# Native fp32 products with plain reads and strided writes, later feed-forward norm sums, and two attention products with other waits

## The chip, the core and the metric

The kernel runs on one core of one Trainium2 chip. The metric is device time in microseconds (us) of one execution. The core's engines are TensorE (PE, matmuls; PEld is its weight load), VectorE (DVE), ScalarE (ACT), GpSimd (POOL) and SyncE (SP, which issues the DMAs). SBUF is the on-chip memory that the engines read, PSUM the eight banks that PE writes.

## The reference

Two transformer-like blocks run one after the other on 256 positions of width 1024, all in fp32. Cut to what matters here:

```python
def hybrid_layer(x, ...):                       # first block
    proj = rms_norm(x, norm1_g) @ w_in
    ...                                         # three attentions, a short convolution, gates
    x = x + mixed @ w_out
    h = rms_norm(x, norm2_g)
    return x + jnp.square(jax.nn.relu(h @ w_up)) @ w_down

def second_block(x, mem, ...):
    z = _rmsnorm(h, norm_mix_g[l]) @ w_in[l]    # conv a and gate, q, k, v, index heads, two gates
    y_conv = _conformer_conv(c_a, c_g, ...) 
    y_attn = _dsa_attention(q, k, v, qi, ki, wi) @ w_attn_out[l]
    h = h + (g_conv * y_conv + g_attn * y_attn) @ w_mix_out[l]
    h = h + _cross_attention(_rmsnorm(h, norm_x_g[l]), _rmsnorm(mem, norm_mem_g[l]), ...)
    hf = _rmsnorm(h, norm_ffn_g[l]) @ w_ff1[l]
    h = h + jnp.square(jax.nn.relu(hf)) @ w_ff2[l]
    return _rmsnorm(h, norm_final_g)
```

The norm in front of each feed-forward half divides every position by the root of its mean square. The kernel multiplies by that factor after the two products, since ReLU and square let a positive factor through; so the factor is needed only when the second product is read out.

## The kernel before, in words

**Weights.** Nearly all weights come as units of 1 MB, 128 partitions by 2048 columns: four blocks of 128 rows of the product by 512 output features. `Stream` loads them through SP's queue in the order of use (line 108), three raw buffers `wr` deep. Each is then split in two: ACT rounds it to fp32r (`wh`, line 125) and DVE subtracts to get the rest (`wl`, line 126), in two halves per unit. Three split buffers exist, and when PE begins a unit the splits of the two units behind it have been asked for. A product of fp32 accuracy is then three fp32r matmuls (`mm3`, lines 261 to 263): high weights by high activations, high by low, low by high.

**Native units.** Four units (`NATIVE`, numbers 81, 85, 89 and 97 in the order) are not split: PE multiplies them in plain fp32 (line 290; line 343 for a token product), which the hardware runs as two matmul instructions per call. All four lie in the second block, where the long convolution loads ACT and DVE: unit 81 is the first half of the first 512 query features, 85 the same of the keys, 89 of the values (the token product), 97 of the second gate.

**Turned columns.** The matmuls of a feature product (`Feat`) read the 256 positions of an activation in the order 0, 128, 1, 129, ... (`turns`) and write PSUM columns one after the other. Whoever reads the PSUM tile out does it through `plain`, which undoes the order. A native unit is the first half of its product; the second half, split, adds onto the same PSUM tile in turned order.

**Order of the work.** PE's order is the order in which the program is written (`manual_schedule`). The other engines' queues are ordered by a planner, by priority and by its own estimate of times; what generators ask for has a priority 400 instructions ahead. Work beside the products is written as Python generators: `pump()` is called twice per unit, after half of it and at its end, and lets each generator run to its next `yield`. A unit is 48 matmuls of 256 columns, so a pump comes every 24 of them. What a generator asks PE for stands in PE's stream at the pump that runs it.

**Feed-forward sums.** `ffn_up` (both blocks) starts `norm_side`, then multiplies with the up weights: the first two groups of 512 features as a pair, the rest one after the other, two units each. `norm_side` asks for the squares and their folds (`sq_sum`, lines 409 to 419: two ACT instructions, four DVE ones) and, some pumps later, for the column sums on PE (`col_stats`, line 427), the scale and power on DVE and POOL, and in the first block, one pump on, for a broadcast by PE (line 457). In the second block `to_tokens` transposes `x` in four steps at the tenth to thirteenth pump, with an ACT copy each (line 1337). The tiles of 4 KB per partition (`H4`) share 24 slots.

**Attention products.** `heads_pv` (line 1010) multiplies transposed probabilities with values for two heads into a bank `po`, from which ACT (line 1015) and DVE (line 1016) make a high and a low half. In the second block's causal attention the loop over eight chunks runs one step per pump beside the gate products; scores (line 1069), transposes (line 1000) four steps later (`LAG2`), and the product with the values one step after those. Its output bank is the one bank of pool `pso`. In the cross attention four such products follow each other directly, in banks of `pss` (three banks) and `pso` by turns; right behind them comes the output projection, which reads `ch`, the halves that they leave. The pool `psm` has four banks, for the large products.

Of the kernel before, what the change touches and what calls it, by code (L numbers as in the profile page):

```python
# [9 lines left out]
F32 = mybir.dt.float32  # L10
# [6 lines left out]
T = 256  # L17
# [130 lines left out]
LAG2 = 4  # L148
# [10 lines left out]
def hybrid_conformer_kernel(ctx, tc, stop, dbg, xT, memT, wall, wtok, wkiwi, wcmp, par_d, cst_d, gfin_d, out):  # L159
    nc = tc.nc  # L160
    V, A, G, P = nc.vector, nc.scalar, nc.gpsimd, nc.tensor
# [4 lines left out]
    psm = ctx.enter_context(tc.tile_pool(name="psm", bufs=4, space=bass.MemoryType.PSUM))  # L166
    pss = ctx.enter_context(tc.tile_pool(name="pss", bufs=3, space=bass.MemoryType.PSUM))
    pso = ctx.enter_context(tc.tile_pool(name="pso", bufs=1, space=bass.MemoryType.PSUM))
# [21 lines left out]
    def PS(name="s"):  # L190
        return pss.tile([128, 512], F32, name=name, tag="s")
# [13 lines left out]
    def turns(ap):  # L205

        return ap.rearrange("p (s a) -> p a s", s=2)

    def plain(ps):

        return ps.rearrange("p n (a s) -> p n s a", s=2)
# [9 lines left out]
    def v3(ap):  # L221
        return ap.rearrange("p (s a) -> p s a", s=2)
# [42 lines left out]
    class Feat:  # L265
# [7 lines left out]
        def chunk(self, c):  # L273
            if self.ps is None:
                self.ps = [psm.tile([128, 2, T], F32, name="m", tag="m") for _ in range(2)]
            ps, act = self.ps, self.act
            wh, wl = W.next()
            wh = wh.rearrange("p (k o) -> p k o", k=4)
            if wl is not None:
                wl = wl.rearrange("p (k o) -> p k o", k=4)  # L280
            ks = self.kts[4 * c:4 * c + 4]
            end = c == self.nch - 1

            def one(kk, o):
                k = ks[kk]
                sl = slice(o * 128, o * 128 + 128)
                first = c == 0 and kk == 0 and o % 2 == 0
                last = end and kk == 3
                if wl is None:
                    P.matmul(out=ps[o // 2][:, o % 2].rearrange("p (a s) -> p a s", s=2), lhsT=wh[:, kk, sl], rhs=turns(act.raw(k)), start=first, stop=last, skip_group_check=True)  # L290
                else:
                    mm3(ps[o // 2][:, o % 2], wh[:, kk, sl], wl[:, kk, sl], act.hi(k), act.lo(k), first, last)

            if not end or self.kmajor:
                for kk in range(4):
                    for o in range(4):
                        one(kk, o)
                    if kk == 1:
                        pump()
                if end:  # L300
                    for b in range(2):
                        self.evac(plain(ps[b]), 2 * b, 2)
            else:
                for b in range(2):
                    for kk in range(4):
                        for o in (2 * b, 2 * b + 1):
                            one(kk, o)
                    self.evac(plain(ps[b]), 2 * b, 2)
                    if b == 0:
                        pump()  # L310
            pump()
# [92 lines left out]
    def sq_sum(src, name):  # L404

        sqs = []
        for hf in range(2):
            sq = H4(name="sq")
            A.activation(out=sq, in_=src[hf], func=AF.Square)
            sqs.append(sq)  # L410
        return fold(sqs)
# [62 lines left out]
    with tc.manual_schedule(engines=MANUAL):  # L474
# [399 lines left out]
        def ffn_up(act, src, tagr, bcast):  # L874
            res = {}

            def norm_side():
                for _ in range(5):
                    yield
                s = sq_sum(src, "s")  # L880
                yield
                yield
                ps = col_stats(s)
                r = rstd_col(ps, D, "r" + tagr)
                r2 = const.tile([128, 2], F32, name="rsq" + tagr)
                V.tensor_tensor(r2, r, r, op=ALU.mult)
                res["col"] = r2
                if not bcast:
                    return
                dg = col_diag(r2)  # L890
                yield
                ps = diag_bcast(dg)
                rb = S([128, T], "rb", 4)
                A.activation(out=rb, in_=ps, func=AF.Copy)
                res["b"] = rb

            res["gen"] = start(norm_side())
            hs = Split([])
            gs = []
            for g in range(8):  # L900
                hs.tiles += HL("hh", 4).tiles

                def ev(ps, o, n, g=g):
                    r = S([128, 2, T], "pr", PR_BUFS)
                    A.activation(out=v4(r), in_=ps, func=AF.Relu)
                    V.tensor_tensor(r, r, r, op=ALU.mult)
                    split_into(hs, r, n, 4 * g + o)

                gs.append(Feat(act, ALL8, ev))
            prod(gs[:2], pair=True)  # L910
            prod(gs[2:])
            return hs, res
# [91 lines left out]

        def heads_pv(pt, nb, v, h0, sp, tt, pool=None):

            po = PS() if pool is pss else pso.tile([128, 512], F32, name="o", tag="o")
            for r in range(2):
                for b in range(nb):
                    P.matmul(out=po[:, r * 128:r * 128 + 128], lhsT=v(b, h0 + r), rhs=pt[:, r, b],  # L1010
                             start=(b == 0), stop=(b == nb - 1))
            tk = slice(tt * 128, tt * 128 + 128)
            o = po[:, 0:256].rearrange("p (r t) -> p r t", r=2)
            h, l = sp.hi(h0, 2)[:, :, tk], sp.lo(h0, 2)[:, :, tk]
            A.activation(out=h, in_=o, func=AF.Copy)
            V.tensor_sub(l, o, h.bitcast(F32))

        def attention2():
# [4 lines left out]
            ps = PS()  # L1023
# [8 lines left out]
            first = [True, True]  # L1032
            for tt in range(2):
                S_ = 128 * (tt + 1)
                for j in range(4):
                    ps = PS()
# [4 lines left out]
                    for hh in range(2):  # L1041
                        h = 2 * j + hh
# [15 lines left out]
                yield  # L1058
            chunks = [(tt, hp) for hp in range(4) for tt in range(2)]
            live = {}  # L1060
            for n in range(len(chunks) + LAG2 + 1):
                if n < len(chunks):
                    tt, hp = chunks[n]
                    S_ = 128 * (tt + 1)
                    tk = slice(tt * 128, tt * 128 + 128)
                    ps = PS()
                    psv = ps.rearrange("p (b s) -> p b s", b=2)
                    for r in range(2):
                        P.matmul(out=psv[:, r, 0:S_], lhsT=at(q2, 2 * hp + r)[:, tk], rhs=at(k2, 2 * hp + r)[:, 0:S_])
                    pr = S([128, 2, T], "pr", PR_BUFS)  # L1070
                    V.scalar_tensor_tensor(out=pr[:, :, 0:S_], in0=psv[:, :, 0:S_], scalar=128.0 ** -0.5, in1=bc(acc[tt], 2),
                                           op0=ALU.mult, op1=ALU.add)
                    mx = S([128, 4], "mx", 5)
                    V.tensor_reduce(out=mx[:, 0:2], in_=pr[:, :, 0:S_], axis=AX, op=ALU.max)
                    V.tensor_scalar(mx[:, 0:2], mx[:, 0:2], -1.0, None, op0=ALU.mult)
                    for r in range(2):
                        A.activation(out=pr[:, r, 0:S_], in_=pr[:, r, 0:S_], func=AF.Exp, bias=mx[:, r:r + 1],
                                     accum_out=mx[:, 2 + r:3 + r])
                    V.reciprocal(mx[:, 2:4], mx[:, 2:4])
                    for r in range(2):  # L1080
                        V.tensor_scalar(pr[:, r, 0:S_], pr[:, r, 0:S_], mx[:, 2 + r:3 + r], None, op0=ALU.mult)
                    live[n] = pr
                m = n - LAG2
                if 0 <= m < len(chunks):
                    live["t", m] = probs_T(live.pop(m), chunks[m][0] + 1)
                m = n - LAG2 - 1
                if m >= 0:
                    tt, hp = chunks[m]
                    heads_pv(live.pop(("t", m)), tt + 1,
                             lambda b, h: v2[b].rearrange("p a c -> p (a c)")[:, 128 * h:128 * h + 128], 2 * hp, as_, tt)  # L1090
                yield
# [78 lines left out]
        for hf in range(2):  # L1170
# [22 lines left out]
            ps = psm.tile([128, 2, T], F32, name="m", tag="m")  # L1193
            wh, wl = W.next()
            for k in range(8):
                sl = slice(128 * k, 128 * k + 128)
# [49 lines left out]
        mems, mem_steps, _ = load_mem()  # L1246
# [35 lines left out]
        cs2 = HL("ch", 4)  # L1282

        def cross():
# [24 lines left out]
                if n == 1:  # L1309
                    yield  # L1310
            for n, (tt, hp) in enumerate(chunks):
                heads_pv(live.pop(("t", n)), 2, lambda b, h: vmf[b][:, 128 * h:128 * h + 128], 2 * hp, cs2, tt, pool=pso if n % 2 else pss)

        cr = start(cross())
        pump()
# [181 lines left out]
```

## Time and profile before

| | |
|---|---|
| median of 3 runs | 923.16 us (922.21 to 924.12) |
| the profiled execution | 920.19 us |
| its span, first to last instruction | 918.1 us |
| PE, DVE, ACT busy | 897.3, 658.5, 546.0 us |
| mean granted clock of PE | 0.994 |

The span is what the trace covers; the profiled execution's own time is 2.1 us longer. "Busy" for PE includes time in which matmuls run at the lower clock. A line number is that of the kernel before; a group such as `L1010` may serve several places, told apart by the tile (`ah` is the causal attention's output, `ch` the cross attention's). In the chain, each piece is followed back to what released it. In a timeline, a group of instructions has its start, its length, and in brackets the idle time before it and what ended that.

### The profile page before, as it was taken

The page shows a single profiled execution, that of the slowest core. Times are in us where ns is not written, and L with a number is a line of the kernel's source. Part 1 is how long each engine was busy: PE and PEld are TensorE (multiplying, and loading weights), DVE is VectorE, ACT ScalarE, POOL GpSimd, SP SyncE. Part 2 cuts the span into 40 slices and gives each one's busy share as a digit, 9 for nine tenths or more (in the row PEclk, how much of TensorE's full clock was granted, in tenths as well). Part 3 has the DMA queues.
Part 4 walks back from the last instruction along what each step waited for, and adds up shares of the span by engine and source line. Part 5 has one row for each costly group of instructions (what it writes and reads, how often), then busy time and mean ns, then how long its engine had stood idle before and what let it go on. Part 6 is the DMA issues. An engine that isn't in the chain of part 4 may idle for free.

```text
span 918.1 us, 17258 instructions
## 1 busy us (share of the span) xinstructions
PE 897.3 (98%) x7238; PEld 857.1 (93%) x7238; DVE 658.5 (72%) x1033; ACT 546.0 (59%) x921; POOL 16.9 (2%) x21
## 2 busy tenths in 40 slices
PE   8999999999989999999999999999999999999996
PEld 8999988999989999999998879989999899998885
DVE  5578898458666775548699988987787675675542
ACT  7534667444556664435696799977566565654432
POOL 0011000000000000000000000000000000000000
PEclk9999999999999999999999999999999999999999
DMA  8754533455545565553553445344565263555541
GB/s 310 282 176 145 200 108 127 147 214 191 187 145 206 199 229 198 212 187 139 205 186 107 172 175 197 126 151 178 204 254 184 93 233 140 195 191 198 214 138 46
DMA packets 25998, 165.00 MB, mean 180 GB/s; under 512 B 3008, under 2 KB 3648, under 8 KB 7360
## 3 DMA queue, kind: packets, MB, share of 16 engines
q1 hardware_dynamic: 25632, 163.38, 50.0%
q8 instruction: 56, 0.92, 0.4%
q10 hardware_dynamic: 288, 0.52, 0.1%
q14 instruction: 22, 0.18, 0.1%
HBM read 162.58 MB, written 1.05 MB: 178 GB/s over the span
## 4 chain that ended last, share of the span: by engine, by line
PE 87%; DVE 6%; ACT 3%; issue 2%; DMA 1%; POOL 0%; SPq 0%; POOLq 0%; DVEq 0%
PE m L261 22%; PE m L263 22%; PE m L262 22%; PE m L346 4%; PE m L347 4%; PE m L348 4%; PE m L290 3%; DVE wl L126 3%; ACT wh L125 1%; PE s L721 1%; PE m L343 1%; DVE y L1119 1%; DMA wr<-in_wall_dram 1%; PE o L761 1%; PE o L1010 1%
## 5 line engine op out<-in xcount | busy, mean ns | idle before, releaser
L126 DVE TENSOR_TENSOR wl<-wr,wh 128x1024 fp32r<-128x1024 f32 (+2 forms) x298 | 348.8, 1195 | 163.3 <-ACT wh L125 163.0
L125 ACT ACTIVATE wh<-wr 128x1024 fp32r<-128x1024 f32 (+2 forms) x298 | 298.4, 1036 | 216.2 <-PE m L262 122.2
L261 PE MATMUL m<-xh,wh 128*128 128x256 f32 x384 | 108.8, 283 | 0.4 <-ACT wh L125 0.4
L263 PE MATMUL m<-xh,wl 128*128 128x256 f32 x384 | 105.9, 276 | 0.9 <-DVE wl L126 0.9
L261 PE MATMUL m<-xnh,wh 128*128 128x256 f32 x376 | 106.7, 284 | 0.0
L262 PE MATMUL m<-xh,wh 128*128 128x256 f32 x384 | 105.8, 276 | 0.2 <-DVE xh L401 0.2
L262 PE MATMUL m<-xnh,wh 128*128 128x256 f32 x376 | 103.5, 275 | 0.0
L263 PE MATMUL m<-xnh,wl 128*128 128x256 f32 x376 | 103.5, 275 | 0.0
L1118 ACT ACTIVATE cp<-u,par 128x255 f32<-128x255 f32 (+23 forms) x192 | 78.7, 489 | 0.0
L261 PEld LDWEIGHTS m<-xh,wh 128*128 128x128 f32 x384 | 73.7, 192 | 2.2 <-issue 1.4
L263 PEld LDWEIGHTS m<-xh,wl 128*128 128x128 f32 x384 | 73.8, 192 | 1.3 <-DVE wl L126 1.3
L262 PEld LDWEIGHTS m<-xh,wh 128*128 128x128 f32 x384 | 73.8, 192 | 0.4 <-DVE xh L401 0.4
L262 PEld LDWEIGHTS m<-xnh,wh 128*128 128x128 f32 x376 | 72.2, 192 | 0.8 <-issue 0.5
L261 PEld LDWEIGHTS m<-xnh,wh 128*128 128x128 f32 x376 | 72.2, 192 | 0.8 <-issue 0.5
L263 PEld LDWEIGHTS m<-xnh,wl 128*128 128x128 f32 x376 | 72.3, 192 | 0.0
L261 PE MATMUL m<-x5h,wh 128*128 128x256 f32 x256 | 71.7, 280 | 0.0
L261 PE MATMUL m<-fh,wh 128*128 128x256 f32 x256 | 71.5, 279 | 0.0
L263 PE MATMUL m<-x5h,wl 128*128 128x256 f32 x256 | 71.3, 278 | 0.0
L262 PE MATMUL m<-x5h,wh 128*128 128x256 f32 x256 | 71.2, 278 | 0.0
L263 PE MATMUL m<-fh,wl 128*128 128x256 f32 x256 | 71.2, 278 | 0.0
L262 PE MATMUL m<-fh,wh 128*128 128x256 f32 x256 | 71.2, 278 | 0.0
L261 PE MATMUL m<-hh,wh 128*128 128x256 f32 x256 | 70.6, 276 | 0.0
(364 smaller groups left out, 2327.5 us busy)
## 6 DMA issues: line engine op xcount, KB each, us to landing
wr<-in_wall_dram SPq DMA_DIRECT2D x145, 1024.0 KB, 4.9
wr<-in_wall_dram SPq DMA_DIRECT2D x8, 256.0 KB, 6.2
mem<-in_memT_dram SPq DMA_DIRECT2D x4, 512.0 KB, 6.2
wr<-in_wtok_dram SPq DMA_DIRECT2D x2, 560.0 KB, 5.2
x<-in_xT_dram SPq DMA_DIRECT2D x4, 256.0 KB, 5.5
wr<-in_wall_dram SPq DMA_DIRECT2D x2, 512.0 KB, 7.5
wck<-in_wcmp_dram SPq DMA_DIRECT2D x2, 512.0 KB, 7.3
cst<-in_cst_dram SPq DMA_DIRECT2D x1, 776.0 KB, 8.9
```

What stands on the lines that cost most here:

```text
L125: self.nc.scalar.activation(out=hi[:, sl], in_=raw[:, sl], func=AF.Copy)
L126: self.nc.vector.tensor_sub(lo[:, sl], raw[:, sl], hi[:, sl].bitcast(F32))
L261: P.matmul(out=ps_ap, lhsT=wh, rhs=xh, start=first, stop=False, skip_group_check=True)
L262: P.matmul(out=ps_ap, lhsT=wh, rhs=xl, start=False, stop=False, skip_group_check=True)
L263: P.matmul(out=ps_ap, lhsT=wl, rhs=xh, start=False, stop=last, skip_group_check=True)
L290: P.matmul(out=ps[o // 2][:, o % 2].rearrange("p (a s) -> p a s", s=2), lhsT=wh[:, kk, sl], rhs=turns(act.raw(k)), start=first, stop=last, ...
L343: P.matmul(out=o, lhsT=act.raw(k)[:, tk], rhs=wh[:, w], start=first, stop=last)
L346: P.matmul(out=o, lhsT=xh, rhs=wh[:, w], start=first, stop=False)
L347: P.matmul(out=o, lhsT=xh, rhs=wl[:, w], start=False, stop=False)
L348: P.matmul(out=o, lhsT=xl, rhs=wh[:, w], start=False, stop=last)
L721: P.matmul(out=psv[:, :, 0:S_], lhsT=q[:, j, tk], rhs=kz[:, g, :, 0:S_])
L1118: A.activation(out=p[:, i, 0:T - d], in_=u[hf][:, i, 0:T - d], func=AF.Copy, scale=w[i])
```

## The change

Three things are edited. The native feature product reads the positions in plain order and writes each to its place in the turned layout, so that its writes step over every second PSUM column. `norm_side` lets nine pumps pass (not five) before the squares, and five (not two) between them and the column sums. `heads_pv` can take a bank of `psm`, which the fourth product of the cross attention does, while its first three take `pss`, `pso`, `pss`; and in the causal attention the product with the values stands two steps behind the transposes, so the loop has one step more.

```diff
--- before.py
+++ after.py
@@ -287,7 +287,7 @@
                 first = c == 0 and kk == 0 and o % 2 == 0
                 last = end and kk == 3
                 if wl is None:
-                    P.matmul(out=ps[o // 2][:, o % 2].rearrange("p (a s) -> p a s", s=2), lhsT=wh[:, kk, sl], rhs=turns(act.raw(k)), start=first, stop=last, skip_group_check=True)
+                    P.matmul(out=plain(ps[o // 2])[:, o % 2], lhsT=wh[:, kk, sl], rhs=v3(act.raw(k)), start=first, stop=last, skip_group_check=True)
                 else:
                     mm3(ps[o // 2][:, o % 2], wh[:, kk, sl], wl[:, kk, sl], act.hi(k), act.lo(k), first, last)
 
@@ -875,11 +875,11 @@
             res = {}
 
             def norm_side():
+                for _ in range(9):
+                    yield
+                s = sq_sum(src, "s")
                 for _ in range(5):
                     yield
-                s = sq_sum(src, "s")
-                yield
-                yield
                 ps = col_stats(s)
                 r = rstd_col(ps, D, "r" + tagr)
                 r2 = const.tile([128, 2], F32, name="rsq" + tagr)
@@ -1004,7 +1004,10 @@
 
         def heads_pv(pt, nb, v, h0, sp, tt, pool=None):
 
-            po = PS() if pool is pss else pso.tile([128, 512], F32, name="o", tag="o")
+            if pool is psm:
+                po = psm.tile([128, 2, T], F32, name="m", tag="m").rearrange("p a t -> p (a t)")
+            else:
+                po = PS() if pool is pss else pso.tile([128, 512], F32, name="o", tag="o")
             for r in range(2):
                 for b in range(nb):
                     P.matmul(out=po[:, r * 128:r * 128 + 128], lhsT=v(b, h0 + r), rhs=pt[:, r, b],
@@ -1058,7 +1061,7 @@
                 yield
             chunks = [(tt, hp) for hp in range(4) for tt in range(2)]
             live = {}
-            for n in range(len(chunks) + LAG2 + 1):
+            for n in range(len(chunks) + LAG2 + 2):
                 if n < len(chunks):
                     tt, hp = chunks[n]
                     S_ = 128 * (tt + 1)
@@ -1083,7 +1086,7 @@
                 m = n - LAG2
                 if 0 <= m < len(chunks):
                     live["t", m] = probs_T(live.pop(m), chunks[m][0] + 1)
-                m = n - LAG2 - 1
+                m = n - LAG2 - 2
                 if m >= 0:
                     tt, hp = chunks[m]
                     heads_pv(live.pop(("t", m)), tt + 1,
@@ -1309,7 +1312,7 @@
                 if n == 1:
                     yield
             for n, (tt, hp) in enumerate(chunks):
-                heads_pv(live.pop(("t", n)), 2, lambda b, h: vmf[b][:, 128 * h:128 * h + 128], 2 * hp, cs2, tt, pool=pso if n % 2 else pss)
+                heads_pv(live.pop(("t", n)), 2, lambda b, h: vmf[b][:, 128 * h:128 * h + 128], 2 * hp, cs2, tt, pool=(pss, pso, pss, psm)[n])
 
         cr = start(cross())
         pump()
```

## Rows read from the trace of the kernel before

**Rows 1.** The page, part 4: shares of the chain that ended last, by engine.

```profile
PE 87%; DVE 6%; ACT 3%; issue 2%; DMA 1%; POOL 0%; SPq 0%; POOLq 0%; DVEq 0%
```

**Rows 2.** Waits of PE: who waited for whom, us in total, times, longest.

```profile
PE s L427 <- DVE sq L419: 3.6, 1, 3.6
PE s L427 <- ACT wh L125: 3.6, 1, 3.6
PE o L1010 <- DVE ch L1016: 1.4, 1, 1.4
PE o L1010 <- DVE ah L1016: 1.3, 1, 1.3
```

**Rows 3.** Busy time by stretch: length, PE, PEld, DVE, ACT, POOL, granted clock, DMA share, GB/s.

```profile
262.55:265.95 3.40, 3.40 (x18) 3.40 (x18) 2.65 (x8) 0.63 (x1) 1.07 (x1) 0.51 0.02 5
760.97:764.30 3.33, 3.33 (x18) 3.33 (x17) 1.58 (x4) 0.63 (x1) 0.69 (x1) 0.50 0.80 288
```

**Rows 4.** Chain from 554 to 592 us: start us, us, what.

```profile
554.40 0.46 issue
...
590.47 1.16 PE o L1010 x8
```

**Rows 5.** Timeline of ACT, first feed-forward block.

```profile
256.58 1.99 ACT L409 ACTIVATE sq<-x 128x1024 f32<-128x1024 f32 x2
```

**Rows 6.** Timeline of DVE, first feed-forward block.

```profile
259.81 0.68 DVE L418 TENSOR_TENSOR sq<-sq 128x512 f32<-128x512 f32 x1
...
264.15 1.22 DVE L126 TENSOR_TENSOR wl<-wr,wh 128x1024 fp32r<-128x1024 f32 x1
...
265.29 0.47 DVE L451 TENSOR_SCALAR diag<-cst,rsqf 128x128 f32<-128x128 f32 x2
```

**Rows 7.** Busy time by stretch, one unit each, in both feed-forward blocks' later groups.

```profile
269.00:274.40 5.40, 5.40 (x51) 5.40 (x50) 3.03 (x3) 2.74 (x4) 0.00 (x0) 1.00 0.09 36
766.90:772.30 5.40, 5.40 (x51) 5.40 (x51) 3.14 (x4) 4.22 (x6) 0.00 (x0) 1.00 0.09 15
```

**Rows 8.** Timeline of PE, first feed-forward block.

```profile
262.11 0.58 PE L427 MATMUL s<-ones,sq 128*128 128x1 f32 x4 [3.60 <-ACT wh L125]
```

**Rows 9.** Chain at four places: split, native plain, native in turns, both again.

```profile
484.09 0.11 PE m L261
...
489.30 0.86 PE s L1038 x2
...
490.16 4.33 PE m L290 x16
...
540.52 8.64 PE m L343 x16
...
594.31 0.87 PE s L1069 x4
```

**Rows 10.** Busy time by stretch, the second block's attention and convolution.

```profile
490.00:554.00 64.00, 64.00 (x395) 52.15 (x394) 59.51 (x105) 51.91 (x108) 0.00 (x0) 1.00 0.50 179
554.00:590.00 36.00, 35.15 (x258) 33.26 (x256) 33.95 (x60) 35.61 (x85) 0.00 (x0) 1.00 0.41 148
590.00:606.00 16.00, 15.53 (x89) 12.71 (x90) 16.00 (x34) 15.07 (x42) 0.00 (x0) 1.00 0.34 120
```

**Rows 11.** Waits of ACT from 484 to 556 us.

```profile
ACT q L1205 <- PE m L263: 4.1, 1, 4.1
...
ACT v L1210 <- PE m L348: 2.1, 2, 1.7
```

**Rows 12.** Timeline of PE, cross attention.

```profile
719.16 1.06 PE L1010 MATMUL o<-pt,vm 128*128 128x128 f32 x8
720.05 1.06 PE L1010 MATMUL s<-pt,vm 128*128 128x128 f32 x8
722.52 1.16 PE L1010 MATMUL o<-pt,vm 128*128 128x128 f32 x8 [1.42 <-DVE ch L1016]
```

**Rows 13.** Timeline of DVE, cross attention.

```profile
722.05 0.42 DVE L1016 TENSOR_TENSOR ch<-o,ch 128x256 fp32r<-128x256 f32 x1
```

## The prediction, made before the changed kernel was run

> **What bounds the kernel now.** I read the page first, then who makes TensorE (PE) wait, then the granted clock around those waits, then the chain and the timelines at each edited place. The chain that ended last is 87% PE [rows 1]: an edit counts if it shortens PE's stream or takes a wait out of it. Of PE's own waits four matter, and the change touches the place of each [rows 2]: 3.6 us and 3.6 us ahead of the column sums of line 427, one in each feed-forward block, and 1.4 us and 1.3 us ahead of attention products of line 1010. For the first of them the trace names ACT's weight split and for the second the last fold of the squares; both had queued behind the squares. The two long ones cost more than they last. [...] From 554.4 to 590.5 us the chain leaves PE for ScalarE (ACT) and VectorE (DVE) and comes back with the 1.3 us wait [rows 4]. So there, and only there over a long stretch, DVE and ACT set the pace.
>
> **The change, part by part.** The sum is against the profiled execution, 920.19 us (span 918.1 and 2.1 around it). It stands 2.97 under the median of 923.16; I add the gain to the median unchanged.
>
> *Feed-forward sums.* Before, squares are asked for at the sixth pump and the column sums stand on PE at the eighth, two half-units of weights (5.3 us of PE) later, in the middle of the first pair's evacuations. After, they are asked for at the tenth pump and stand at the fifteenth, 13.3 us of PE later. What moves, in each block: two squares on ACT (2 us with [rows 5]), four folds on DVE (one is 0.68 [rows 6], the last half as long), four column sums on PE, then the small scale and power work; no DMA is in it. Nothing is added. The folds ended about 9 us after they were asked for (5.3 plus 3.6), so 13.3 us cover them with 4 us over, more if the new place is quieter. It is: in units of the later groups ACT is busy 2.74 and 4.22 us of 5.40 and DVE 3.03 and 3.14 [rows 7], so 2 us of squares and some 2.5 of folds fit in the gaps of two units. What queues behind the squares on ACT is the weight split `wh`, which runs two units (10.7 us) ahead of PE; 2 us do not use that up. In the second block the squares meet the four copies of line 1337, which the 4.22 us contain two of; if cover were gone there PE would lose at most the 2 us of squares. The tiles hold: with `x`, `x5h`, `x5t`, `gfin`, the squares and four groups' `hs`, 2 + 4 + 2 + 1 + 2 + 8 = 19 of 24 slots are in use. Gain: 3.60 + 3.40 x 0.49 = 5.27 and 3.61 + 3.33 x 0.50 = 5.28, together **10.5 us**. Against it, in the first block, the broadcast product of line 457 follows the sums by one pump, which at full clock is 24 matmuls, 2.7 us, plus 0.4 for the sums. Its chain took from 262.11 [rows 8] to about 265.7 us, 3.6, with a 1.1 us weight split in it [rows 6]; without that it is 2.4. So PE waits 0 to 0.5 us: I take 0.3. Net **-10.2**, bounds -10.5 and -8 (no wait at 457; the 2 us of squares uncovered once).
>
> *Native products.* Three units (81, 85, 97) of 32 matmul instructions change; the fourth native unit, 89, is a token product with its own reading in turns and stays. Sixteen take 4.33 us, so 0.271 us for 256 columns [rows 9]. The fourth unit: 8.64 us for 16 of 512 columns, 1.055 ns a column, the same. Native products that read plain columns and write plain ones need 0.86 us for two of 512 and 0.87 for four of 256, 0.84 ns a column or 0.217 us per 256 [rows 9]. They load fresh weights each time and one kind stands between the two halves of a native unit, so the order of reading is the difference I see. No row has a write with gaps. The low end is that it is free: 0.217. The high end is a write at half the column rate; the nearest row for any matmul at half rate is the split product under the half clock [rows 3], so 2 x 0.217 = 0.434. I take 0.217, because the new form shares engine mode, size and reading with that row and differs in one thing. Raw: 96 x (0.271 - 0.217) = **-5.2**; at the high end 96 x 0.163 = +15.6.
>
> How much of -5.2 is kept? Units 81 and 85 (1.7 us each) lie ahead of the stretch that ACT and DVE pace. DVE is busy 59.51 of 64 us before 554, then 33.95 of 36 and 16.00 of 16 [rows 10]. ACT waits for PE's results in the first part, 4.1 and 2.1 us at the longest [rows 11], so an earlier PE lets ACT start earlier; DVE has 4.5 us of gaps to follow. I keep 2.5 of 3.4 (bounds 0 and 3.4). Unit 97 lies where DVE is full: I keep 1.0 of 1.7. Together **-3.5**.
>
> [...]
>
> *The second block's causal attention.* The product now stands two pumps behind its transposes, not one. The wait is for the single `pso` bank, held until DVE's line 1016 had read the product before it [rows 2]. At 590.5 the first product now stands, on a free bank, so the 1.3 goes; next late is the same bank one pump on, where DVE is as full. The loop takes one step more, at the fourteenth of sixteen pumps, so nothing waits for it. I take **-0.7**, bounds -1.3 and 0.
>
> *Cross attention.* The fourth product takes a `psm` bank and does not wait for the second's. It stood from 722.52, after 1.42 us of waiting [rows 12]; now it follows the third. One product is 0.89 us (719.16 to 720.05). But the output projection behind it needs the same low half, ready at 722.47 [rows 13], in its second matmul. So PE fills the wait with 0.89 + 0.11 and still waits 0.4: **-1.0**, bounds -1.4 and 0. The four `psm` banks hold: two for the query product are read out by then.
>
> Sum: -10.2 - 3.5 - 0.7 - 1.0 = **-15.4**: 904.8 for the profiled run, **907.7** for the median.
>
> **The rivals.** (a) *The write with gaps halves the column rate.* For it: no row shows such a write. Against: a native instruction spends 0.217 us on 256 columns where a split one spends 0.11, which may leave the write its time. Place: units 81, 85, 97; price +15.6; the 1.3 us wait at 590 goes too, as DVE gains slack: -10.2 - 1.0 - 1.3 + 15.6 = +3.1, **926.3**. It decides if one instruction costs over about 0.41 us (then 96 x 0.144 eats the 12 us of the other parts and 1.8 more). [...] (b) *The write takes back what the read gives.* An instruction stays near 0.271, or the reading was not the cause: -10.2 - 0.7 - 1.0 = -11.9, **911.3**. For it: TensorE still has two orders to reconcile, as now. A milder loss, 0.32 us, would give 916. (c) *The sums stay late.* The squares are placed behind other work by the planner, and PE waits at the new place, or the weight split behind them comes late; half of -10.2 remains: **912.8**. Against: the gaps of [rows 7]. (d) *The pace of DVE takes the native gain.* All but 1 us of -5.2 comes back as a longer wait near 590: -10.2 - 1.0 - 0.7 - 1.0 = -12.9, **910.3**. For it: [rows 10]. Against: the chain passes through PE up to 554.4.
>
> **How the numbers follow.** Chances: forecast 0.48 (its own range 904 to 909.5), (a) 0.12, (b) 0.18, (c) 0.10, (d) 0.12. The low end is every part in full, 923.16 - 18.4 = 904.8, less 0.8 for reordering by the planner: 904. The high end takes in (b), (c), (d) and the milder loss: 917. That leaves out (a) and little else, some 0.15. A measurement of this kernel tells about 0.2%, 1.8 us, from no change. Faster by more: all but (a) and a few hundredths of mishaps; 0.86. Same: 0.04, which is (a) at part of its price. Slower: 0.10.
>
> **What would show it.** Right: line 427 is gone from PE's waits, the granted clock is 1.00 after both first pairs, native instructions follow each other at 0.217 us, the fourth cross product starts right behind the third, and the wait left at line 1016 is under 1 us. Wrong: native instructions at 0.27 or over 0.4; a new wait of PE for `wh` or `wl` in the third or fourth group of a feed-forward block; line 457 waiting over 1 us; a PE wait of 2 us or more between 570 and 606.

## The result, and the profile after

The changed kernel takes 908.28 us (median of 4 runs, 905.11 to 910.44) against 922.68 us (4 runs, 921.91 to 924.12) of the kernel before on the same chip: a ratio of 0.9839 [0.9804, 0.9875], 14.4 us less. The forecast was 907.7 us. The total came out within 0.6 us; the parts did not, as the runs below show: two gains were larger than forecast, one part cost time, and the errors nearly cancelled. The four executions spread over 5.3 us, so an agreement to 0.6 is luck.

The profiled execution of the changed kernel took 909.66 us. From its page, the span, the busy times and the shares of the chain that ended last, which answer to [rows 1]:

```profile
span 907.7 us, 17260 instructions
...
PE 892.1 (98%) x7238; PEld 856.8 (94%) x7238; DVE 658.6 (73%) x1033; ACT 545.1 (60%) x921; POOL 16.9 (2%) x21
...
PE 87%; DVE 7%; ACT 2%; issue 1%; DMA 1%; SPq 1%; POOL 0%; POOLq 0%; DVEq 0%; ACTq 0%
```

TensorE still sets the time. Its waits (who waited for whom, us in total, times, longest) answer to [rows 2]; lines behind the edits of `ffn_up` and `heads_pv` have moved on by three, so 1010 is now 1013 and 1016 is 1019:

```profile
PE o L1013 <- DVE ah L1019: 3.2, 2, 2.2
PE m L261 <- ACT wh L125: 1.7, 1, 1.7
...
PE m L262 <- DVE ch L1019: 0.4, 1, 0.4
```

The two waits of 3.6 us at line 427 are gone, and of the 1.4 us in the cross attention 0.4 is left. The causal attention, which had one wait of 1.3 us, now has two that sum to 3.2. The 1.7 for ACT's weight split lies in start-up, at 16 us, ahead of all that was edited. Busy time by stretch shows the clock where the sums were (first two lines: first block; third: second block) and behind the new wait (last line), against [rows 3]:

```profile
252.00:262.00 10.00, 10.00 (x92) 10.00 (x91) 7.84 (x9) 6.28 (x9) 0.00 (x0) 1.00 0.48 167
262.00:285.00 23.00, 23.00 (x209) 23.00 (x208) 18.39 (x26) 16.01 (x22) 1.07 (x1) 1.00 0.61 217
752.00:775.00 23.00, 23.00 (x209) 23.00 (x208) 17.07 (x23) 16.15 (x23) 1.07 (x1) 1.00 0.53 191
...
614.40:618.50 4.10, 4.09 (x22) 4.09 (x23) 3.58 (x5) 1.44 (x3) 0.00 (x0) 0.58 0.00 0
```

PE is busy without a gap and at a granted clock of 1.00 past both first pairs; the half clock now stands at 614 us and, in this execution, in start-up (below). In the chain, the native units, against [rows 9] (start, us, instructions):

```profile
487.86 3.45 PE m L290 x16
...
511.71 6.91 PE m L290 x32
...
534.69 8.64 PE m L343 x16
```

Sixteen native instructions take 3.45 us, not 4.33, so 0.216 us each: the plain read's price, with nothing on top for the write (E7 compares this directly). Unit 89 (line 343), which the change leaves alone, takes its 8.64 as before.

**Where the time went, by stretch.** I cut each execution at events that all kernels have: the first broadcast of line 457 (just after start-up), that of the memory's norm, the first scores of the cross attention, and the first transposes of `to_tokens` (near 402, 708 and 767 us in the kernel before). The first cut takes out start-up, which moves by 3 us between executions of one code: 27.82 us before, 31.01 in the changed kernel, 30.25 in the first experiment (E1), which has the same code there. Its trace shows what moves it: PE's first long wait for a weight split, at 16 us, and the clock behind it. Before the change and after it (columns as above):

```profile
17.50:24.30 6.80, 6.24 (x55) 6.12 (x55) 3.59 (x6) 4.92 (x7) 0.70 (x1) 1.00 0.88 344
17.50:24.30 6.80, 6.29 (x29) 5.86 (x28) 3.44 (x5) 2.42 (x4) 0.00 (x0) 0.50 0.89 331
```

Here 6.80 us at 0.50 cost 3.4 us. So it is in all twelve profiles: in five, with waits of 0.4 to 0.93 us there, the clock stayed at 1.00 and start-up took 27.8 to 28.5 us; in seven, with waits of 1.19 to 1.75 us, half clock followed, for 3.4 us in five (29.3 to 30.3) and for 6.8 us in two (31.0). In us of the profiled executions, as differences from before:

| kernel | first block | attention stretch | cross attention, first pair of feed-forward | rest |
|---|---|---|---|---|
| before, length | 374.18 | 306.03 | 59.09 | 150.98 |
| the change | -5.49 | -1.61 | -6.93 | +0.44 |
| sums alone | -5.47 | +0.03 | -5.93 | +0.44 |
| native products alone | -0.03 | -5.26 | +1.52 | +0.09 |
| lag alone | +1.61 | +3.68 | +1.23 | +0.08 |
| cross attention alone | +1.61 | +0.02 | -1.02 | +0.05 |
| change without the lag | -5.49 | -5.26 | -6.92 | +0.52 |

The 0.44 in the last column is no loss: the four sums of the second block (0.34 us in the chain) now stand behind the cut instead of ahead of it. (The cuts are read from the chain, to about 0.1 us; by the starts of PE's own instructions that column is 0.44 wherever the sums are late and 0.00 elsewhere.) The entries of +1.2 to +1.6 are longer half clocks behind the old 3.6 us waits; E2 and E4 show them. Within the stretches the parts add up: -5.26 + 3.68 = -1.58 against -1.61.

### The profile page after: what moved, and what is told of

It reads as the page before. It is cut to its first block, busy times and chain, and to the rows that moved or that the text cites. A ratio compares the mean times of both kernels' runs of the same rounds, so it can differ in the third digit from the quotient of the medians.

```text
span 907.7 us, 17260 instructions
## 1 busy us (share of the span) xinstructions
PE 892.1 (98%) x7238; PEld 856.8 (94%) x7238; DVE 658.6 (73%) x1033; ACT 545.1 (60%) x921; POOL 16.9 (2%) x21
## 4 chain that ended last, share of the span: by engine, by line
PE 87%; DVE 7%; ACT 2%; issue 1%; DMA 1%; SPq 1%; POOL 0%; POOLq 0%; DVEq 0%; ACTq 0%
PE m L261 23%; PE m L262 22%; PE m L263 22%; PE m L346 4%; PE m L347 4%; PE m L348 4%; DVE wl L126 3%; PE m L290 2%; PE s L721 1%; PE m L343 1%; DMA x<-in_xT_dram 1%; DVE y L1122 1%; PE o L761 1%; ACT wh L125 1%; PE o L1013 1%
## 5 line engine op out<-in xcount | busy, mean ns | idle before, releaser
L261 PE MATMUL m<-xh,wh 128*128 128x256 f32 x384 | 110.0, 286 | 1.7 <-ACT wh L125 1.7
L262 PE MATMUL m<-xh,wh 128*128 128x256 f32 x384 | 107.1, 279 | 0.2 <-DVE xh L401 0.2
L261 PEld LDWEIGHTS m<-xh,wh 128*128 128x128 f32 x384 | 74.9, 195 | 3.5 <-ACT wh L125 1.8
L262 PEld LDWEIGHTS m<-xh,wh 128*128 128x128 f32 x384 | 74.9, 195 | 0.4 <-DVE xh L401 0.4
L261 PE MATMUL m<-x5h,wh 128*128 128x256 f32 x256 | 70.8, 277 | 0.0
L261 PE MATMUL m<-hh,wh 128*128 128x256 f32 x256 | 70.6, 276 | 0.0
L262 PE MATMUL m<-hh,wh 128*128 128x256 f32 x256 | 70.4, 275 | 0.0
L263 PE MATMUL m<-hh,wl 128*128 128x256 f32 x256 | 70.4, 275 | 0.0
```

Of the source, the lines that this page charges most:

```text
L261: P.matmul(out=ps_ap, lhsT=wh, rhs=xh, start=first, stop=False, skip_group_check=True)
L262: P.matmul(out=ps_ap, lhsT=wh, rhs=xl, start=False, stop=False, skip_group_check=True)
L263: P.matmul(out=ps_ap, lhsT=wl, rhs=xh, start=False, stop=last, skip_group_check=True)
```

## The experiments

They carry the names of their runs; there is no E6. Each of the first four keeps one part of the change and undoes the rest; differences of medians are against runs of the kernel before on the same chip.

**E1. The sums alone.**

```diff
             def norm_side():
+                for _ in range(9):
+                    yield
+                s = sq_sum(src, "s")
                 for _ in range(5):
                     yield
-                s = sq_sum(src, "s")
-                yield
-                yield
```

> The kernel before with the later feed-forward sums alone. My theory: both waits at line 427 and both half-clock stretches go and nothing comes in their place but 0.4 us at line 457, so 10 to 10.5 us less. Rival (the sums stay late, or what queues behind the squares does): 5 us less or fewer, with a new wait of PE for a weight split in the third or fourth group.

Measured: 911.23 us (910.21 to 911.71) against 923.6 (19 runs), 0.9862 [0.9843, 0.9881], so -12.4. The stretches of the profiles give -5.47 in the first block and -5.93 + 0.44 = -5.49 in the second, 11.0 together. Its waits show the gap closed; behind them, the place of the longest:

```profile
PE m L261 <- ACT wh L125: 1.7, 1, 1.7
PE o L1010 <- DVE ch L1016: 1.4, 1, 1.4
PE o L1010 <- DVE ah L1016: 1.3, 1, 1.3
...
PE s L457 <- DVE diag L451: 0.4, 1, 0.4
```

```profile
16.46 0.38 PE L261 MATMUL m<-xh,wh 128*128 128x256 f32 x1 [1.75 <-ACT wh L125]
```

That 1.7 is not the weight split of the rival: it stands in start-up, and the kernel before waits 0.4 there. Around the sums nothing new came: PE is busy for all of 252 to 285 and 752 to 780 us, at 1.00. The 0.4 at line 457 is an older one of the first norm: E4, with the sums as before, has it too. The medians give more than the profiles because the profile of before was one of the cheap cases, as E4 shows.

**E2. The native products alone.**

```diff
-                    P.matmul(out=ps[o // 2][:, o % 2].rearrange("p (a s) -> p a s", s=2), lhsT=wh[:, kk, sl], rhs=turns(act.raw(k)), start=first, stop=last, skip_group_check=True)
+                    P.matmul(out=plain(ps[o // 2])[:, o % 2], lhsT=wh[:, kk, sl], rhs=v3(act.raw(k)), start=first, stop=last, skip_group_check=True)
```

> The kernel before with the native products' new order alone. Theory A (the gain of 96 x 0.055 us stays, and what the changed kernel loses near 614 us is the longer lag's doing): 4.5 to 5.3 us less, and no PE wait of over 1.5 us between 570 and 630 us. Theory B (DVE's pace takes the gain, whatever the lag): 1 to 2.5 us less, with 3 us or more of PE waits for line 1016 in that stretch.

Measured: 918.59 us (917.02 to 919.8), 0.9943 [0.9925, 0.9962], so -5.0; by stretch -5.26 where the units are, and next to nothing elsewhere but +1.52 behind. There the 3.6 us wait of before still stands, and here it is followed by 6.7 us at half clock, not the 3.33 of [rows 3]; then, second line, the stretch of the units, to compare with the first line of [rows 10]:

```profile
756.50:763.20 6.70, 6.67 (x31) 6.70 (x32) 3.23 (x6) 0.63 (x1) 1.07 (x1) 0.50 0.45 157
492.36:552.91 60.55, 60.55 (x395) 52.21 (x394) 58.19 (x101) 51.40 (x108) 0.00 (x0) 1.00 0.49 178
```

For the same 395 matmuls DVE's gaps shrank from 4.5 to 2.4 us: it followed PE. In the chain, sixteen again take

```profile
492.52 3.45 PE m L290 x16
```

So 96 instructions save 96 x (0.271 - 0.216) = 5.3 us, and all of it is kept. The waits of before at line 427, near 590 us and in the cross attention are still there at their size:

```profile
PE s L427 <- DVE sq L419: 3.6, 1, 3.6
PE s L427 <- ACT wh L125: 3.6, 1, 3.6
...
PE o L1010 <- DVE ch L1016: 1.4, 1, 1.4
PE o L1010 <- DVE ah L1016: 1.3, 1, 1.3
```

**E3. The lag of the causal attention alone.**

```diff
-            for n in range(len(chunks) + LAG2 + 1):
+            for n in range(len(chunks) + LAG2 + 2):
...
-                m = n - LAG2 - 1
+                m = n - LAG2 - 2
```

> The kernel before with the causal attention's product one pump later, alone. Theory A: the last product now stands behind the read-out of the one before it, which queues behind the long convolution's mean and squares; PE waits about 2 us there and the clock falls after it, so 2 to 4 us more in all, though the wait near 590 shrinks by 0.3. Theory B (the lag is harmless, DVE's pace under a faster PE is what costs): 0 to 1.3 us less and no wait of over 1 us near 617.

Measured: 926.86 us (10 runs, 923.5 to 928.2), 1.0033 [1.0018, 1.0048]: 3.3 us slower. The wait that it was to remove is still there, and a longer one has come (PE's timeline, with the idle time before each and what ended it; then the window behind the second):

```profile
597.25 1.16 PE L1010 MATMUL o<-pt,v 128*128 128x128 f32 x8 [1.00 <-DVE ah L1016]
...
625.11 1.77 PE L1010 MATMUL o<-pt,v 128*128 128x128 f32 x8 [2.19 <-DVE ah L1016]
```

```profile
626.00:629.00 3.00, 3.00 (x17) 3.00 (x16) 2.45 (x4) 0.54 (x2) 0.00 (x0) 0.52 0.00 0
```

The first wait shrank from 1.32 to 1.00 us. The eighth and last product waits 2.19 us, and after that gap the granted clock is 0.52 over the 3.00 us of the window.

**E4. The cross attention alone.**

```diff
-                heads_pv(live.pop(("t", n)), 2, lambda b, h: vmf[b][:, 128 * h:128 * h + 128], 2 * hp, cs2, tt, pool=pso if n % 2 else pss)
+                heads_pv(live.pop(("t", n)), 2, lambda b, h: vmf[b][:, 128 * h:128 * h + 128], 2 * hp, cs2, tt, pool=(pss, pso, pss, psm)[n])
```

> The kernel before with the cross attention's fourth product in a bank of the large products, alone. By the step of the prediction: 1.0 us less, with 0.4 us of wait left in the output projection's second matmul. Rival (the bank is late, or the projection waits as long): no change within 0.3 us.

Measured: 922.35 us (10 runs, 919.88 to 924.27), 0.9983 [0.9971, 0.9996], so -1.25, and -1.02 by stretch. In the first block this kernel equals the one before, and yet it takes 1.61 us longer there, as E3 does. The windows behind its 3.6 us wait show why:

```profile
262.75:266.15 3.40, 3.40 (x16) 3.40 (x17) 2.24 (x5) 0.63 (x1) 1.07 (x1) 0.50 0.02 5
266.15:269.50 3.35, 3.35 (x18) 3.35 (x18) 1.25 (x4) 0.00 (x0) 0.00 (x0) 0.50 0.60 198
```

The half clock lasts 6.75 us here, not 3.40 as in [rows 3]: 3.35 us more at 0.50 are 1.7 us lost. (E2 above has the same in the second block.) The same wait of 3.6 us costs 5.3 us in one execution and 7.0 in another. So the sums are worth 11 us against the one profile and 12.4 against the median.

**E5. The change without the lag.** The other three parts stay.

```diff
-            for n in range(len(chunks) + LAG2 + 2):
+            for n in range(len(chunks) + LAG2 + 1):
...
-                m = n - LAG2 - 2
+                m = n - LAG2 - 1
```

> The changed kernel with the causal attention's product put back one pump behind its transposes. Theory A (the lag costs about 2.2 us of wait and 1.7 us of half clock near 614): 3 to 4 us less than the changed kernel, 902 to 905, with one wait of 1 to 2.5 us near 585. Theory B (DVE's pace takes the native gain whatever the lag): within 1 us of the changed kernel, with waits of 3 us or more in the same stretch.

Measured: 903.25 us (902.74 to 905.65) against 923.42 (7 runs), 0.9789 [0.9761, 0.9816], so -20.2. The attention stretch is 3.65 us shorter than the changed kernel's. One wait is left at line 1013:

```profile
PE o L1013 <- DVE ah L1019: 1.3, 1, 1.3
```

So the lag, which alone costs 3.3 us of median, costs its 3.7 us of stretch beside the other parts too.

**E7. Split products in plain order.** On top of the change, the split products read plain columns and write plain ones, the PSUM layout is plain, and the native products read and write without gaps.

```diff
     def plain(ps):
-        return ps.rearrange("p n (a s) -> p n s a", s=2)
+        return ps.rearrange("p n (s a) -> p n s a", s=2)
...
     def mm3(ps_ap, wh, wl, xh, xl, first, last):
-        ps_ap = ps_ap.rearrange("p (a s) -> p a s", s=2)
-        xh, xl = turns(xh), turns(xl)
+        ps_ap = v3(ps_ap)
+        xh, xl = v3(xh), v3(xl)
```

> The changed kernel with every feature product, split and native, reading plain columns and writing plain ones. It asks what the turned order is worth to the split products. If the order of reading only matters to native ones: the split matmul stays at 0.111 us per 256 columns, the native one at 0.216, and the time stays within 2 us. If split products need the turned order: they slow down to between 0.14 (as the native ones did, by a quarter) and 0.22 us (half rate), which over some 5000 of them is 140 to 550 us more.

Measured: 942.18 us (942.01 and 942.35), 1.0202 [1.017, 1.0234]. Native units take 3.45 us per sixteen here too, where they write without gaps: this is the direct comparison, and the strided write of the change costs nothing that shows. The split products pay for the plain order. PE's timeline, the first and the last of 49 in a row:

```profile
295.96 0.28 PE L261 MATMUL m<-fh,wh 128*128 128x256 f32 x1
...
301.64 0.28 PE L261 MATMUL m<-fh,wh 128*128 128x256 f32 x1
```

(The 0.28 is one matmul from start to modelled end; they overlap, so the pace is the distance of starts.) That is 5.68 / 48 = 0.118 us. The changed kernel, in turned order, takes 5.36 / 48 = 0.112 for 49 of the same product:

```profile
284.18 0.28 PE L261 MATMUL m<-fh,wh 128*128 128x256 f32 x1
...
289.54 0.28 PE L261 MATMUL m<-fh,wh 128*128 128x256 f32 x1
```

There are 5928 of them, so up to 40 us; 33 us of span show against the changed kernel, and 36 behind start-up, which was 2.8 us shorter here. Turned reading helps the split products by 6% and hurts the native ones by 25% (0.271 to 0.216).

**E8. The token unit too.** The native token product (unit 89) gets the same form: plain read, strided write.

```diff
-                    P.matmul(out=o, lhsT=act.raw(k)[:, tk], rhs=wh[:, w], start=first, stop=last)
+                    P.matmul(out=o.rearrange("p a s -> p s a"), lhsT=act.raw(k)[:, tk], rhs=wh[:, w].rearrange("p a s -> p s a"), start=first, stop=last)
```

> The changed kernel with the one native token product (unit 89) also reading plain columns and writing strided ones. If a strided write is free at 512 columns too: its 16 instructions take 6.9 us in place of 8.64, and the kernel up to 1.7 us less. If the strided write costs there: 8.64 or more.

Measured: 906.38 us (906.36 and 906.4), 0.9814 [0.9783, 0.9845]. In the chain the unit falls from 8.64 to

```profile
533.18 6.87 PE m L343 x16
```

which is 0.43 us for 512 columns, again the plain pace. The attention stretch is 1.94 us shorter than the changed kernel's, which looks like the unit's 1.77, but isn't. Its waits, and the window behind the 2.2 us wait (PE's product at 612.59):

```profile
PE o L1013 <- DVE ah L1019: 3.4, 2, 2.2
...
PE s L1000 <- DVE pr L1074: 0.7, 1, 0.7
```

```profile
612.60:617.60 5.00, 5.00 (x44) 5.00 (x45) 3.50 (x5) 2.22 (x5) 0.00 (x0) 1.00 0.12 18
```

In this execution the clock stayed at 1.00 behind the same 2.2 us wait; that alone saves the 1.7 us that the changed kernel lost there (4.10 x 0.42). So of the unit's own 1.77 only some 0.2 was kept (1.94 - 1.7). Waits for DVE took 0.2 more at line 1013 and 0.7 new at the transposes; the rest, some 0.6, is not in the list of waits.

**E9. The convolution's norm one pump later.** If the last product is late because its predecessor is read out behind the norm's squares on ACT, moving the norm behind that read must remove the wait, with the lag left as the change has it.

```diff
                     V.tensor_tensor(s[:, 0], s[:, 0], s[:, 1], op=ALU.add)
             yield
+            yield
             ps = PS()
             P.matmul(out=ps[:, 0:T], lhsT=ones, rhs=s[:, 0])
```

> The changed kernel, lag kept, with the long convolution's layer norm asked for one pump later, so that the seventh causal product's read-out no longer stands behind its mean and squares. If that queue is why the lag costs (my theory): the 2.2 us wait of the last product and the half clock after it go, and the stretch from the memory norm's broadcast to the cross attention shrinks by 3.5 to 4 us; about 904. If the lag costs in another way (the last product's read-out itself is late, or DVE's pace): within 1 us of the changed kernel, the wait still there.

Measured: 903.98 us (902.42 to 904.64) against 922.85 (7 runs), 0.9792 [0.9776, 0.9809]; the attention stretch is 5.96 us shorter than before's, 4.35 shorter than the changed kernel's. First its waits, then the window, then ACT's timeline at the place:

```profile
PE o L1013 <- DVE ah L1019: 1.0, 1, 1.0
```

```profile
600.00:625.00 25.00, 25.00 (x225) 24.95 (x224) 19.84 (x30) 16.50 (x28) 0.69 (x1) 1.00 0.57 211
```

```profile
612.22 0.38 ACT L1018 ACTIVATE ah<-o 128x256 fp32r<-128x256 f32 x1
613.78 1.06 ACT L1147 ACTIVATE sq<-y 128x1024 f32<-128x1024 f32 x1 [1.19 <-DVE y L1145]
```

Both the 2.2 us wait and the half clock are gone: 25 us of PE without a gap at 1.00. With the queue clear, lag and later norm together are worth 5.96 - 5.26 = 0.7 us in the stretch against E5. That this is the figure forecast for the lag is luck: the wait of 1.3 us was to go and fell by 0.35, and the other 0.35 is spread over small differences that were not traced. The medians, 903.98 and 903.25, cannot tell the two kernels apart.

**E10 and E11. The token unit without the lag, and with the later norm.** E8's edit on top of E5, and on top of E9; no other edits.

> The changed kernel without the longer lag and with the token product's strided write too, the two gains that the runs so far showed. If they add: 1.5 to 1.8 us less than without the lag alone, so 901 to 902. If DVE's pace now binds near 585: the wait at line 1019 there grows from 1.3 to 3 us and nothing is gained.

> The changed kernel with the layer norm one pump later and the token product's strided write. By the theory of the queue the longer lag is then worth its 0.3 us at the wait near 585: within 0.5 us of the variant without the lag, 901 to 902. Otherwise as the changed kernel less 1.7 at best, 905 or more.

Measured: 905.26 us (902.02 to 908.22), 0.9797 [0.9772, 0.9822], and 903.56 us (902.15 to 904.71), 0.9789 [0.9772, 0.9807]. Neither beats its base by the median, though unit 89 is 1.77 us shorter in both. E10's timeline of PE, then the windows behind it:

```profile
584.34 2.08 PE L1013 MATMUL o<-pt,v 128*128 128x128 f32 x8 [1.98 <-DVE ah L1019]
```

```profile
584.30:587.00 2.70, 2.66 (x12) 2.67 (x13) 2.70 (x6) 2.52 (x8) 0.00 (x0) 0.50 0.00 0
587.00:590.00 3.00, 3.00 (x25) 2.95 (x24) 2.89 (x12) 3.00 (x11) 0.00 (x0) 0.90 0.63 188
```

PE reaches the second product earlier, waits 1.98 us instead of 1.3, and then runs at 0.50 and 0.90: 1.35 + 0.3 = 1.65 us lost. The attention stretch is 1.15 us longer than in E5. In E11 the wait at line 1013 goes from 1.0 to 1.2 and one of 0.7 appears at the transposes; 0.3 us of the 1.77 is kept. So in all three kernels with the token unit this is rival (d), one step later than I had placed it: once PE is 5.3 us ahead, the next 1.8 us meet the pace of DVE. It rests on one profile for each, and of the loss in E10 some 0.6 us is left, of which 0.2 is a wait at the transposes and the rest isn't traced.

## Why the prediction was right, and where its steps were wrong

**Sums: right mechanism, too small.** Forecast -10.2; 11.0 by stretch, 12.4 by median. Waits and half clock went as said, the gaps of [rows 7] held the squares and folds, so rival (c) falls, and the broadcast at line 457 did not wait: the 0.3 was never paid. The term that was mis-sized is "3.60 + 3.40 x 0.49": a length of the half clock read from one execution, the first line of [rows 3]. In another it lasted twice as long (6.75 us, E4), so the step "I add the gain to the median unchanged" missed some 1.4 us.

**Native: right price, wrong share.** The instruction went to 0.216 us (forecast 0.217); rivals (a) and (b) fall by that row alone. The step that failed is "I keep 2.5 of 3.4" and "I keep 1.0 of 1.7": all of the raw 5.2 was kept (5.26). DVE's 59.51 of 64 us [rows 10] was taken as a brake, but in E2 its gaps shrank and no wait of PE there grew. Nor did DVE set the pace up to 590 us, as the chain of [rows 4] was read: PE was busy there for 35.15 of 36.00 us [rows 10], and in E2 the wait at its end is 1.3 us still, though the product behind it starts 3.5 us earlier, counted from the first cut (559.12 us, 562.65 before). The runs with the token unit show where that margin ends. That a write with gaps could take 0.434 us an instruction, the high end, was an estimate that no run bears out: sixteen took 3.45 us with gaps in the changed kernel and 3.45 without them in E7. Reading in turns costs the native product (0.271 against 0.216) and helps the split one (0.112 turned, 0.118 plain); why was not shown.

**Lag: wrong sign.** Forecast -0.7, bounds -1.3 and 0; measured +3.7. The failing step is "the loop takes one step more, at the fourteenth of sixteen pumps, so nothing waits for it". I looked at the pump where the last product stands on PE, and not at what stands on ACT between it and the product ahead, whose read-out frees the one bank. The changed kernel's timelines of PE, ACT and DVE:

```profile
608.93 0.61 PE L1013 MATMUL o<-pt,v 128*128 128x128 f32 x4
...
614.41 1.75 PE L1013 MATMUL o<-pt,v 128*128 128x128 f32 x8 [2.19 <-DVE ah L1019]
```

```profile
611.16 2.13 ACT L1146 ACTIVATE sq<-y 128x1024 f32<-128x1024 f32 x2 [3.35 <-DVE y L1144]
613.20 0.36 ACT L1018 ACTIVATE ah<-o 128x256 fp32r<-128x256 f32 x1
```

```profile
609.85 2.36 DVE L1144 TENSOR_TENSOR y<-y,rb 128x1024 f32<-128x1024 f32 x2
...
613.94 0.42 DVE L1019 TENSOR_TENSOR ah<-o,ah 128x256 fp32r<-128x256 f32 x1
```

The seventh product is done at 609.5. ACT stands idle for 3.35 us, at the head of its queue the squares of the layer norm, which wait for DVE to subtract the mean; then they take 2.13, and only then comes `ah`. PE stops for 2.19 us and runs 4.10 us at 0.58, which is 2.19 + 4.10 x 0.42 = 3.9, less 0.3 for the wait that shrank. (In E8 only the clock's part of it stayed away. Not every execution of the changed kernel seems to have had that part either: the one of 905.11 us shows a mean granted clock of 0.998, the same as E5's profile, where the clock is 1.00 from 582.6 to 625 us; the changed kernel's profile shows 0.993.) Before, both last read-outs stood ahead of those squares: ACT's timeline of the kernel before has

```profile
614.57 0.37 ACT L1015 ACTIVATE ah<-o 128x256 fp32r<-128x256 f32 x1
...
618.38 0.39 ACT L1015 ACTIVATE ah<-o 128x256 fp32r<-128x256 f32 x1 [1.76 <-PE o L1010]
619.56 1.06 ACT L1143 ACTIVATE sq<-y 128x1024 f32<-128x1024 f32 x1 [0.79 <-DVE y L1141]
```

E9 moved only that neighbour, and the wait went: shown, not just argued. The prediction had named "a PE wait of 2 us or more between 570 and 606" as a sign that it was wrong; the wait came, 8 us later.

**Cross attention: right.** Forecast -1.0, measured -1.0 by stretch, and the 0.4 us that were to be left are left.

Over all: by medians -12.4 - 5.0 + 3.3 - 1.25 = -15.35, measured -14.4. The forecast of -15.4 was 2.2 and 1.5 too small in two parts and 4 too large in a third. That the total fits is luck; what was right is the mechanism of the sums, of the native instruction and of the cross attention.

**Open.** Why PE's wait at 16 us differs between executions of one code was not traced; with the clock behind it, it spreads single runs of one kernel by 3 us. What sets how long the half clock lasts after the same wait, and why it stayed away in E8, was not settled either.

## What to carry to other kernels

Before a product is moved later on PE, follow the read-out that frees its bank through ACT's and DVE's queues: here the product was done at 609.5 us, and ACT read it out only at 613.20, behind squares that had waited 3.35 us for DVE and took 2.13. Price a PE wait with the low clock behind it (behind the same 3.6 us it was about 0.50 for 3.4 or for 6.75 us), and take that from several executions. The best kernels here leave the lag out or move the norm behind it: 903.25 and 903.98 us (E11: 903.56), 2.1% under the one before.

## What the runs showed that was not expected

A native fp32 matmul wants the opposite order from a split one: 0.216 us for 256 columns read plain against 0.271 in turns, while a split product takes 0.118 plain and 0.112 in turns. Writing every second PSUM column cost the native product nothing that shows: 3.45 us per sixteen with gaps, and 3.45 without (E7). And the clock behind a wait is not one price: 3.6 us of waiting was followed by 3.4 or 6.75 us at about 0.50 of the clock, 2.2 us by 0.58 over 4.10 us or by 1.00 over 5.00 us (E8), 1.98 us by 0.50 over 2.70 us and 0.90 over the next 3.00 (E10), while behind the waits of 1.0 and 1.3 us at the same product the profiles of the change and of E5 and E9 show 1.00. In start-up, where PE had shorter waits around it, waits of 1.19 to 1.75 us were followed by 3.4 or 6.8 us at about 0.50.
